# Attention values for four query blocks at once, in a fixed scheme over score steps

## The chip, the cores and the metric

The kernel runs on one core of a Trainium2 chip. The metric is device time in microseconds (us) of one execution. Engines are named as the profile names them: PE is TensorE's matmuls, PEld its weight loads, DVE VectorE, ACT ScalarE, POOL GpSimd and SP SyncE. POOL and SP issue DMAs here; POOL computes almost nothing.

## The reference

A small decoder trunk over 1,024 tokens of width 1,024, in float32: one short-convolution layer with a feed-forward part, then one layer of latent attention (8 heads) with a feed-forward part, then a norm. The change touches only the attention:

```
kv = (c_lat @ w_ukv)            # per head: 128 key columns, 128 value columns
q  = (cq @ w_uq)                # per head: 128 plain columns, 64 rotary columns
sc = q_nope . k_nope + q_pe . k_pe          # per block of 128 queries
p  = softmax(where(causal mask, sc * scale, -big))
attn = p @ v                                # per head
h  = h + attn @ w_o
```

With causal masking, query block qb (0 to 7, of 128 rows each) sees key blocks 0 to qb.

## The kernel before

Every float32 operand is split into two float32r parts, hi and lo (`split`, L93: a cast on ACT, L95, and a subtraction on DVE, L96). A product is three matmuls: hi by hi, hi by lo, lo by hi. Feature-major layout is used throughout: tokens lie along the free dimension, up to 512 columns for one matmul.

For each head h, four things are made ahead by projections: `make_k` (keys, 12 matmuls of 512 columns), `make_q` (plain queries, 18 of 512), and for two heads at a time `make_qr` (rotary queries, 18 of 512, then four rotary operations queued one by one and `done`, which moves the parts into place with DMAs on POOL) and `make_v` (values, 48 of 256). `wsplit` (L861) loads a projection's weights with a DMA on SP and splits them.

`scores` (L939) makes one query block: five terms in up to two pieces of 512 columns, a mask matmul (L948), a maximum on DVE (L950, L951), the exponential on ACT (L953, with its sum), and the scaling of the row on DVE (L954, L955). A score tile takes one PSUM bank (`ps1`, four buffers) up to 512 columns and two banks (`ps2`, two buffers) above. Projections use `ps2` too.

`pv` (L958) takes two query blocks (2i and 2i+1). It transposes their rows by key block on PE (L973, L974), two key blocks into one `ps1` bank, splits the bank into a `pt` tile (L95, L96), and then multiplies for each of its 2i+2 key blocks the value block's two parts with the 256 columns (128 at the last key block): L985, L986, L987. The output, 256 columns in its own `ps1` bank, is split, and stored to the DRAM tile `od` by POOL (`move`, L88), or kept in SBUF for the last two heads (`Od`).

The loop at L1036 runs over heads and over i = 0 to 3. Each round emits the scores of two blocks, then `pv` of the pair made two rounds earlier (`DEPTH` = 2), then a projection as the table `PLACES` (L40) says. In head 6 the outputs of heads 0 and 1 are loaded back (O0), in head 7 those of heads 2 to 5 (O1, eight loads of 512 KB on POOL, L1049). In these two heads `project_o` also makes the early part of the output projection, from heads 0 and 1, for all eight output blocks n, adding each into the residual block `h_of(n)`, which is itself loaded by a DMA on POOL. The remaining part follows after the loop (L1073).

SBUF tiles of 4 KB per partition come from one pool of 41 (`slot`). A planner orders the emitted instructions on each engine: the order of emission is their priority, and it takes those first that its own timing model holds to be ready. It also places all waits. On the chip each engine then runs its list in that order.

Of the kernel before, what the change touches and what calls it, by code (L numbers as in the profile page):

```python
# [10 lines left out]
F32 = mybir.dt.float32  # L11
F32R = mybir.dt.float32r
# [12 lines left out]
H = 8  # L25
# [2 lines left out]
QL = 384  # L28
EPS = 1e-6
SCALE = float((128 + ROPE) ** -0.5)  # L30
DEPTH = 2
NSLOT = 41
NHALF = 6
NRAW = 10
# [2 lines left out]
EARLY = 2  # L37
GROUPS = ((0, 1), (2, 3, 4), (5, 6, 7), (8, 9, 10))
KEPT = 4
PLACES = {0: ((0,), (1,), (), ()), 6: ((0,), (1,), (2, 3), (4,)), 7: ((0,), (1, 2), (3,), (4,))}  # L40
PLACES.update({h: ((0,), (1,), (2,), (3,)) if h % 2 else ((), (0,), (1,), ()) for h in range(1, 6)})
PREFETCH = 4
TC = {"schedule_with_timeline_sim": True}

# [13 lines left out]
def trunk(ctx, tc, aps, out):  # L58
# [22 lines left out]
    def ps2(name):  # L81
        return psum.tile([P, S], F32, name=name, tag="ps2", bufs=2)
# [786 lines left out]

    def make_k(h):  # L870
        w = wsplit("wk", w_ukv[:, :, h, 0:P], [P, 2, P])
        ps = ps2("ps_k")
        gemm(ps, w, lambda k: ch[k], lambda k: cl[k], range(2))
        kh, kl = slot("kh", F32R), slot("kl", F32R)
        split(kh, kl, ps)
        Kt[h] = (kh, kl)

    def make_v(h):

        raw = wraw("wv")  # L880
        dst = raw.rearrange("p (k h m) -> p k h m", k=2, h=2)
        for k in range(2):
            nc.sync.dma_start(dst[:, k], w_ukv[:, k, h:h + 2, P:2 * P])
        hi, lo = part(wop("wv"))
        split(hi, lo, raw)
        wh, wl = [t.rearrange("p (k m) -> p k m", k=2) for t in (hi, lo)]
        Vt[h], Vt[h + 1] = [(slot("vh", F32R), slot("vl", F32R)) for _ in range(2)]
        for t4 in range(2):
            ps = ps2("ps_v")
            for tb in range(4):  # L890
                tok = slice((t4 * 4 + tb) * P, (t4 * 4 + tb + 1) * P)
                o = ps[:, tb * 256:(tb + 1) * 256]
                for k in range(2):
                    nc.tensor.matmul(o, lhsT=ch[k][:, tok], rhs=wh[:, k, :], start=k == 0, stop=False)
                    nc.tensor.matmul(o, lhsT=ch[k][:, tok], rhs=wl[:, k, :], start=False, stop=False)
                    nc.tensor.matmul(o, lhsT=cl[k][:, tok], rhs=wh[:, k, :], start=False, stop=k == 1)
            pv_ = ps.rearrange("p (t h d) -> p t h d", h=2, d=P)
            for h2 in range(2):
                ov = lambda t: t[:, t4 * 512:(t4 + 1) * 512].rearrange("p (t d) -> p t d", d=P)
                split(ov(Vt[h + h2][0]), ov(Vt[h + h2][1]), pv_[:, :, h2, :])  # L900

    def make_q(h):
        w = wsplit("wqn", w_uq[:, :, h, 0:P], [P, 3, P])
        ps = ps2("ps_q")
        gemm(ps, w, lambda k: qh[k], lambda k: ql[k], range(3))
        a, b = slot("qnh", F32R), slot("qnl", F32R)
        split(a, b, ps)
        Qt.setdefault(h, {}).update(h=a, l=b)

    def make_qr(h):  # L910
# [6 lines left out]
        for k in range(3):  # L917
            rp = lambda t: t[:, k * P:(k + 1) * P].rearrange("p (q h f) -> p h q f", q=2, h=2, f=32)
            split(rp(hi), rp(lo), raw[:, k * P:(k + 1) * P].rearrange("p (h q f) -> p h q f", h=2, q=2, f=32))
        ps = ps2("ps_q")  # L920
        gemm(ps, lambda k: (hi[:, k * P:(k + 1) * P], lo[:, k * P:(k + 1) * P]),
             lambda k: qh[k], lambda k: ql[k], range(3))
# [16 lines left out]
    def scores(K, Q, qb, p):  # L939
        kw = (qb + 1) * P  # L940
        ps = ps2("ps_s") if kw > 512 else ps1("ps_s1")
        qs = slice(qb * P, kw)
        terms = ((Q["h"], K[0]), (Q["h"], K[1]), (Q["l"], K[0]), (Q["r"], KH), (Q["r"], KL))
        for i, (q, k) in enumerate(terms):
            for a in range(0, kw, 512):
                b = min(kw, a + 512)
                nc.tensor.matmul(ps[:, a:b], lhsT=q[:, qs], rhs=k[:, a:b], start=i == 0, stop=i == 4 and b < kw)  # L947
        nc.tensor.matmul(ps[:, qb * P:kw], lhsT=identr, rhs=cmask, start=False, stop=True)  # L948
        mx = small.tile([P, 1], F32, name="mx", bufs=4)
        nc.vector.reduce_max(mx, ps[:, :kw], axis=AX.X)  # L950
        nc.vector.tensor_scalar(mx, mx, nqscale[:, qb:qb + 1], None, ALU.mult)  # L951
        rsum = small.tile([P, 1], F32, name="rsum", bufs=4)
        nc.scalar.activation(p, ps[:, :kw], AF.Exp, bias=mx, scale=qscale[:, qb:qb + 1], accum_out=rsum)  # L953
        nc.vector.reciprocal(rsum, rsum)  # L954
        nc.vector.tensor_scalar(p, p, rsum, None, ALU.mult)  # L955
        return p

    def pv(V, i, pa, pb, h):  # L958
        nb = 2 * i + 2
        o = ps1("ps_pv")  # L960
        PT = []
        for _ in range(0, nb, 2):
            t = slot("pt", F32R)
            PT.append([t[:, a].rearrange("p (k q) -> p k q", q=256) for a in (T1, T2)])
        for kb in range(0, nb, 2):
            t = ps1("ps_t")
            tv = t.rearrange("p (k q) -> p k q", q=256)
            h_, l_ = PT[kb // 2]
            last = kb == nb - 2
            for j in range(2):  # L970
                ks = slice((kb + j) * P, (kb + j + 1) * P)
                if not (last and j == 1):
                    nc.tensor.transpose(tv[:, j, 0:P], pa[:, ks], ident)  # L973
                nc.tensor.transpose(tv[:, j, P:256], pb[:, ks], ident)  # L974
            if last:
                split(h_[:, 0, :], l_[:, 0, :], tv[:, 0, :])
                split(h_[:, 1, P:], l_[:, 1, P:], tv[:, 1, P:])
            else:
                split(h_, l_, tv)
        for kb in range(nb):  # L980
            h_, l_ = PT[kb // 2]
            vs = slice(kb * P, (kb + 1) * P)
            cs = slice(P, 256) if kb == nb - 1 else slice(0, 256)
            f, e = kb == 0, kb == nb - 1
            nc.tensor.matmul(o[:, cs], lhsT=V[0][:, vs], rhs=h_[:, kb % 2, cs], start=f, stop=False)  # L985
            nc.tensor.matmul(o[:, cs], lhsT=V[0][:, vs], rhs=l_[:, kb % 2, cs], start=False, stop=False)  # L986
            nc.tensor.matmul(o[:, cs], lhsT=V[1][:, vs], rhs=h_[:, kb % 2, cs], start=False, stop=e)  # L987
        if h in Od:
            split(Od[h][0][:, i * 256:(i + 1) * 256], Od[h][1][:, i * 256:(i + 1) * 256], o[:, :256])
            return  # L990
        ot = half("oh", F32R)
        oh, ol = ot[:, :256], ot[:, 256:]
        split(oh, ol, o[:, :256])
        move(od[h, 0, :, i * 256:(i + 1) * 256], oh)
        move(od[h, 1, :, i * 256:(i + 1) * 256], ol)

    make_k(0)
    make_qr(0)
    drip()
    make_q(0)  # L1000
    make_v(0)
    rq = rstd(q_acc, QL, pre=get_rs())
    qscale, nqscale = [const.tile([P, NT], F32, name=n) for n in ("qscale", "nqscale")]
    nc.vector.tensor_scalar(qscale, rq, SCALE, None, ALU.mult)
# [9 lines left out]

    st, h_of = stream(move)

    def project_o(O, k0, n):

        ps = ps2("ps_wo")
# [4 lines left out]
        hn = h_of(n)  # L1024
        nc.vector.tensor_tensor(hn, ps, hn, ALU.add)

    def p_tiles(i):
        a, b = (2 * i + 1) * P, (2 * i + 2) * P
        if a + b <= S:
            t = slot("p")  # L1030
            return t[:, :a], t[:, a:a + b]
        return slot("p")[:, :a], slot("p")[:, :b]

    Od = {}
    pend = []
    for h in range(H):  # L1036
        if h >= 6:
            Od[h] = (slot("oth", F32R), slot("otl", F32R))
        jobs = []
        if h + 1 < H:  # L1040
            jobs = [lambda h=h: make_k(h + 1), lambda h=h: make_q(h + 1)]
            if h % 2:
                jobs = [lambda: make_qr(h + 1), lambda: make_v(h + 1)] + jobs
        if h == H - 2:
            O0 = [load_o(k) for k in range(EARLY)]
        if h == H - 1:
            for n in range(3, 5):
                h_of(n)
            O1 = [load_o(k) for k in range(EARLY, 6)] + [Od[6], Od[7]]  # L1049
        if h >= H - 2:  # L1050
            early = range(KD)[:3] if h == H - 2 else range(KD)[3:]
            for n in early[:2]:
                h_of(n)
            jobs += [lambda n=n: project_o(O0, 0, n) for n in early]
        per = PLACES[h]
        for i in range(4):
            pa, pb = p_tiles(i)
            if i == 0:
                drip()
            for qb, p in ((2 * i, pa), (2 * i + 1, pb)):  # L1060
                scores(Kt[h], Qt[h], qb, p)
                drip(1)
            if len(pend) == DEPTH:
                pv(*pend.pop(0))
            pend.append((Vt[h], i, pa, pb, h))
            for j in per[i]:
                jobs[j]()
    for u in pend:
        pv(*u)


    X, final = next_operands(st, "mla_ffn_norm_g")
    for n in range(KD):  # L1073
# [104 lines left out]
```

## Time and profile before

| | us |
|---|---|
| median of three runs | 2125.18 (2120.62 to 2125.85) |
| the profiled execution, whole | 2121.5 |
| its span, first to last instruction | 2119.7 |
| PE busy | 2077.5 |
| DVE busy | 1627.7 |
| ACT busy | 935.5 |
| attention stage (1082.7 to 1403.1 of the span) | 320.4 |

In the profile a line gives an engine, a line of the kernel, an operation with output<-inputs (buffer numbers left out), and a count. Busy times of PE come from modelled ends of pipelined matmuls, so the spacing of starts says more than the durations. A wait is put down to the instruction that released it.

### The profile page before, as it was taken

What the parts mean: (1) busy time and instruction counts of PE and PEld (TensorE: products, weight loads), DVE (VectorE), ACT (ScalarE), POOL (GpSimd) and SP (SyncE); (2) the same over time, 40 slices, a digit from 0 to 9 for tenths busy, and PEclk for the clock granted to TensorE, in tenths of its full rate; (3) what the DMA queues carried; (4) which work ended last, traced back from release to release, by engine and by line L of the source; (5) the groups of instructions that cost most, each with busy time, mean ns of one, the idle gap of its engine ahead of it and who ended that gap; (6) DMA issues with size and microseconds to landing.
All of it is one profiled execution on the core that took longest, in us unless ns stands there. A gap on an engine that the chain in (4) does not pass through costs nothing.

```text
span 2119.7 us, 27634 instructions
## 1 busy us (share of the span) xinstructions
PE 2077.5 (98%) x9798; PEld 1730.1 (82%) x9798; DVE 1627.7 (77%) x2694; ACT 935.5 (44%) x1729; POOL 245.2 (12%) x464
## 2 busy tenths in 40 slices
PE   8999999999999999999999999999999999999998
PEld 6878887888888878888888888887888888878886
DVE  5697757789988887689467767767888888887785
ACT  6633344444444453224345545445444444443235
POOL 1000100000101121110002022100001010121100
PEclk9999999999999999999999999999999999999998
DMA  6133462343545587865222124522445445685851
GB/s 246 35 96 119 145 208 92 122 147 127 179 139 168 178 305 236 272 220 156 62 52 68 38 63 124 170 82 85 128 134 175 141 159 154 199 285 195 292 186 80
DMA packets 266858, 321.28 MB, mean 152 GB/s; under 512 B 19343, under 2 KB 214096, under 8 KB 266720
## 3 DMA queue, kind: packets, MB, share of 16 engines
q0 software_dynamic: 61248, 201.46, 28.1%
q1 hardware_dynamic: 205472, 118.07, 19.0%
q8 instruction: 77, 1.26, 0.2%
q14 instruction: 61, 0.50, 0.1%
HBM read 206.22 MB, written 108.00 MB: 148 GB/s over the span
## 4 chain that ended last, share of the span: by engine, by line
PE 88%; DVE 6%; DMA 2%; ACT 2%; issue 2%; SPq 0%; POOL 0%; POOLq 0%; ACTq 0%; DVEq 0%
PE ps_z L183 35%; PE ps_y L183 26%; PE ps_c L228 7%; PE ps_s L947 4%; PE ps_wo L108 1%; PE ps_wo L110 1%; PE ps_wo L112 1%; PE ps_l L112 1%; PE ps_l L108 1%; PE ps_l L110 1%; PE ps_pv L985 1%; PE ps_pv L986 1%; DMA w<-in_conv_ffn_w_dram 1%; PE ps_pv L987 1%; PE ps_q L108 1%
## 5 line engine op out<-in xcount | busy, mean ns | idle before, releaser
L183 PE MATMUL ps_z<-x,wo 128*128 128x512 f32 x2532 | 608.7, 389 | 3.6 <-ACT z L197 2.8
L183 PEld LDWEIGHTS ps_z<-x,wo 128*128 128x128 f32 x2532 | 474.6, 188 | 104.4 <-ACT z L197 4.1
L183 PE MATMUL ps_y<-x,wo 128*128 128x512 f32 x1764 | 432.3, 389 | 1.2 <-DVE x L96 0.9
L183 PEld LDWEIGHTS ps_y<-x,wo 128*128 128x128 f32 x1764 | 330.5, 188 | 70.9 <-DVE x L96 1.8
L95 ACT CAST wo<-w 128x512 fp32r<-128x512 f32 (+2 forms) x423 | 238.7, 570 | 278.0 <-PE ps_z L183 109.0
L96 DVE TENSOR_TENSOR wo<-w,wo 128x512 fp32r<-128x512 f32 (+2 forms) x423 | 260.4, 622 | 61.9 <-ACT wo L95 61.0
L183 PE MATMUL ps_z<-xm,wo 128*128 128x512 f32 x960 | 239.0, 392 | 4.2 <-ACT wo L95 1.6
L183 PEld LDWEIGHTS ps_z<-xm,wo 128*128 128x128 f32 x960 | 178.6, 188 | 46.3 <-DVE h L503 3.4
L95 ACT CAST wo<-sums 128x512 fp32r<-128x512 f32 (+2 forms) x172 | 98.3, 572 | 256.7 <-PE ps_y L183 101.5
L183 PE MATMUL ps_y<-xm,wo 128*128 128x512 f32 x720 | 181.6, 390 | 2.0 <-DVE h L503 2.0
L88 POOL DMA_DIRECT2D md<-x x140 | 74.9, 536 | 737.8 <-DVE x L96 704.8
L183 PEld LDWEIGHTS ps_y<-xm,wo 128*128 128x128 f32 x720 | 134.7, 188 | 31.0 <-DVE h L503 2.9
L197 ACT COPY z<-ps_z 128x512 f32<-128x512 f32 x106 | 62.0, 585 | 136.6 <-PE ps_z L183 136.5
L96 DVE TENSOR_TENSOR wo<-sums,wo 128x512 fp32r<-128x512 f32 (+2 forms) x172 | 107.2, 623 | 14.3 <-ACT wo L95 12.7
L88 POOL DMA_DIRECT2D xm<-md x140 | 74.1, 535 | 251.3 <-PE ps_z L183 126.3
L503 DVE TENSOR_TENSOR h<-ps_z,h 128x512 f32<-128x512 f32 x104 | 71.4, 687 | 36.5 <-PE ps_z L183 35.7
L96 DVE TENSOR_TENSOR x<-t,x 128x512 fp32r<-128x512 f32 x136 | 92.0, 684 | 5.1 <-ACT x L95 5.1
L237 DVE TENSOR_TENSOR a<-ps_y,z 128x512 f32<-128x512 f32 x88 | 60.6, 688 | 42.4 <-PE ps_y L183 42.1
L95 ACT CAST x<-t 128x512 fp32r<-128x512 f32 x136 | 82.4, 621 | 20.9 <-DVE t L252 20.3
L953 ACT ACTIVATE p<-ps_s,mx,qscale 128x128 f32<-128x128 f32 (+3 forms) x64 | 53.4, 835 | 82.4 <-DVE mx L951 80.0
L158 DVE TENSOR_TENSOR sums<-w,w 128x512 f32<-128x512 f32 (+2 forms) x85 | 53.2, 626 | 29.4 <-DMA w<-in_mla_ffn_w_dram 13.4
L503 DVE TENSOR_TENSOR h<-ps_y,h 128x512 f32<-128x512 f32 x88 | 60.2, 685 | 19.9 <-PE ps_y L183 19.8
(297 smaller groups left out, 3344.8 us busy)
## 6 DMA issues: line engine op xcount, KB each, us to landing
md<-x POOLq DMA_DIRECT2D x140, 512.0 KB, 3.6
xm<-md POOLq DMA_DIRECT2D x140, 512.0 KB, 8.1
w<-in_conv_ffn_w_dram SPq DMA_DIRECT2D x88, 256.0 KB, 2.8
w<-in_mla_ffn_w_dram SPq DMA_DIRECT2D x88, 256.0 KB, 3.0
w<-in_conv_w_in_dram SPq DMA_DIRECT2D x48, 256.0 KB, 3.0
hd<-h POOLq DMA_DIRECT2D x24, 512.0 KB, 3.6
w<-in_conv_ffn_w_dram SPq DMA_DIRECT2D x48, 192.0 KB, 4.9
w<-in_mla_ffn_w_dram SPq DMA_DIRECT2D x48, 192.0 KB, 4.5
```

The costliest lines, as they stand in the source:

```text
L88: nc.gpsimd.dma_start(dst, src)
L95: nc.scalar.copy(out=hi, in_=src)
L96: (eng or nc.vector).tensor_tensor(lo, src, hi.bitcast(F32), ALU.subtract)
L108: nc.tensor.matmul(ps[:, hs], lhsT=wh, rhs=xh(k)[:, hs], start=st, stop=False)
L158: tt(sums, R["12"], R["22"], ALU.add)
L183: mm = lambda w_, x_, f: nc.tensor.matmul(b, lhsT=w_[:, m], rhs=x_, start=f, stop=True, skip_group_check=True)
L197: nc.scalar.copy(out=kept[name], in_=b)
L228: nc.tensor.matmul(ps[:, ts], lhsT=w_[:, m], rhs=X[i][f"b{kh}{th}"][:, q, :], start=st and j == 0, stop=en and j == 2)
L237: nc.vector.tensor_tensor(dst, ps, add, ALU.add)
L503: nc.vector.tensor_tensor(dst[name], b, dst[name], ALU.add)
L947: nc.tensor.matmul(ps[:, a:b], lhsT=q[:, qs], rhs=k[:, a:b], start=i == 0, stop=i == 4 and b < kw)
L953: nc.scalar.activation(p, ps[:, :kw], AF.Exp, bias=mx, scale=qscale[:, qb:qb + 1], accum_out=rsum)
```

## The change

`pv` is split into three functions that the loop calls piecemeal. A group g is four query blocks: group 0 is blocks 0 to 3 with four key blocks, group 1 blocks 4 to 7 with eight. `turn(kb)` transposes key block kb of all query blocks that see it into one bank and returns the function that splits it. `add(kb)` does the three matmuls for one key block, with 512 columns (384, 256, 128 on the diagonal). `out_` splits 512 output columns. The loop runs over steps t = 8h + qb; two key blocks are turned in each step from the second after a group's last scores, and added two steps later. `scores` now returns the exponential part and the scaling, which the loop emits a step later. Projections are generators: the part up to the first `yield` (weight load and split, and for an early output part the load of its residual block) is emitted a step ahead of the rest. They stand at set steps: in even heads keys at block 0 and queries at block 2; in odd heads rotary queries at 0, values at 1 and 2, keys at 3, queries at 6. The early output parts stand at three steps of head 6, three of head 7, and two after it.

```diff
-DEPTH = 2
-PLACES = {0: ((0,), (1,), (), ()), 6: ((0,), (1,), (2, 3), (4,)), 7: ((0,), (1, 2), (3,), (4,))}
-PLACES.update({h: ((0,), (1,), (2,), (3,)) if h % 2 else ((), (0,), (1,), ()) for h in range(1, 6)})
...
     def make_k(h):
         w = wsplit("wk", w_ukv[:, :, h, 0:P], [P, 2, P])
+        yield
         ps = ps2("ps_k")
...
         for t4 in range(2):
+            yield
             ps = ps2("ps_v")
...
-        mx = small.tile([P, 1], F32, name="mx", bufs=4)
-        nc.vector.reduce_max(mx, ps[:, :kw], axis=AX.X)
-        nc.vector.tensor_scalar(mx, mx, nqscale[:, qb:qb + 1], None, ALU.mult)
-        rsum = small.tile([P, 1], F32, name="rsum", bufs=4)
-        nc.scalar.activation(p, ps[:, :kw], AF.Exp, bias=mx, scale=qscale[:, qb:qb + 1], accum_out=rsum)
-        nc.vector.reciprocal(rsum, rsum)
-        nc.vector.tensor_scalar(p, p, rsum, None, ALU.mult)
-        return p
-
-    def pv(V, i, pa, pb, h):
...
+        mx, rsum = [small.tile([P, 1], F32, name=n, bufs=4) for n in ("mx", "rsum")]
+
+        def exp():
+            nc.vector.reduce_max(mx, ps[:, :kw], axis=AX.X)
+            nc.vector.tensor_scalar(mx, mx, nqscale[:, qb:qb + 1], None, ALU.mult)
+            nc.scalar.activation(p, ps[:, :kw], AF.Exp, bias=mx, scale=qscale[:, qb:qb + 1], accum_out=rsum)
+
+        def scaled():
+            nc.vector.reciprocal(rsum, rsum)
+            nc.vector.tensor_scalar(p, p, rsum, None, ALU.mult)
+
+        return exp, scaled
+
+    def pv(V, g, p, h):
+
+        nb, q0 = 4 * g + 4, 4 * g
+        PT, O = {}, []
+
+        def turn(kb):
+            t, o_ = ps1("ps_t"), slot("pt", F32R, [P, 2, HS])
+            j0 = max(0, kb - q0)
+            for j in range(j0, 4):
+                nc.tensor.transpose(t[:, j * P:(j + 1) * P], p[j][:, kb * P:(kb + 1) * P], ident)
+            cs = slice(j0 * P, HS)
+            PT[kb] = o_, cs
+            return lambda: split(o_[:, 0, cs], o_[:, 1, cs], t[:, cs])
+
+        def add(kb):
+            if kb == 0:
+                O.append(ps1("ps_pv"))
+            o, (o_, cs) = O[0], PT.pop(kb)
+            vs = slice(kb * P, (kb + 1) * P)
+            for i, (v, q) in enumerate(((0, 0), (0, 1), (1, 0))):
+                nc.tensor.matmul(o[:, cs], lhsT=V[v][:, vs], rhs=o_[:, q, cs], start=kb == 0 and i == 0, stop=kb == nb - 1 and i == 2)
+
+        def out_():
+            ts = (T1, T2)[g]
+            if h in Od:
+                split(Od[h][0][:, ts], Od[h][1][:, ts], O[0])
             else:
...
+                oh, ol = half("oh", F32R), half("ol", F32R)
+                split(oh, ol, O[0])
+                move(od[h, 0, :, ts], oh)
+                move(od[h, 1, :, ts], ol)
+
+        return turn, add, out_
...
+    def project_early(n):
+        hn = h_of(n)
+        w = wsplit("wo", w_o[:, 0:EARLY, n * P:(n + 1) * P], [P, EARLY, P])
+        yield
+        ps = ps2("ps_wo")
+        gemm(ps, w, lambda k: O0[k][0], lambda k: O0[k][1], range(EARLY))
+        nc.vector.tensor_tensor(hn, ps, hn, ALU.add)
...
+    def place(h, qb, job):
+
+        t = h * NT + qb
+        jobs.setdefault(t - 1, []).append(job)
+        for i in range(2 if job.gi_code.co_name == "make_v" else 1):
+            jobs.setdefault(t + i, []).append(job)
+
+    for h in range(H - 1):
+        if h % 2:
+            for qb, job in enumerate((make_qr(h + 1), make_v(h + 1))):
+                place(h, qb, job)
+        place(h, 3 if h % 2 else 0, make_k(h + 1))
+        place(h, 6 if h % 2 else 2, make_q(h + 1))
+    for n, (h, qb) in enumerate(((6, 3), (6, 5), (6, 7), (7, 0), (7, 1), (7, 2), (8, 0), (8, 1))):
+        place(h, qb, project_early(n))
...
+    for t in range(H * NT + 7):
+        h, qb = t // NT, t % NT
+        if h < H:
...
+            exp, scaled = scores(Kt[h], Qt[h], qb, p[qb % 4])
+        for f in splits:
+            f()
+        splits = []
+        if h < H:
+            exp()
+        now = units.pop(t, ())
+        for f in now:
+            if f[0] == "turn":
+                splits.append(f[1]())
+        for f in now:
+            if f[0] == "add":
+                f[1]()
+        if last_scaled:
+            last_scaled()
+        last_scaled = scaled if h < H else None
+        for f in now:
+            if f[0] == "out":
+                f[1]()
+        drip(1)
+        run_jobs(t)
+        if qb % 4 == 3 and h < H:
+            turn, add, out_ = pv(Vt[h], qb // 4, p, h)
+            nb = 4 * (qb // 4) + 4
+            for kb in range(nb):
+                units.setdefault(t + 2 + kb // 2, []).append(("turn", lambda kb=kb, f=turn: f(kb)))
+            for kb in range(nb):
+                units.setdefault(t + 4 + kb // 2, []).append(("add", lambda kb=kb, f=add: f(kb)))
+            units[t + 3 + nb // 2].append(("out", out_))
```

## Rows read from the trace of the kernel before

**Rows 1.** The page, parts 1 and 4: busy time, chain that ended last.

```profile
PE 2077.5 (98%) x9798; PEld 1730.1 (82%) x9798; DVE 1627.7 (77%) x2694; ACT 935.5 (44%) x1729; POOL 245.2 (12%) x464
...
PE 88%; DVE 6%; DMA 2%; ACT 2%; issue 2%; SPq 0%; POOL 0%; POOLq 0%; ACTq 0%; DVEq 0%
```

**Rows 2.** Busy time by stretch: from:to, length, each engine busy (instructions), clock, DMA.

```profile
1082.70:1131.06 48.36, 47.64 (x317) 43.21 (x315) 37.22 (x95) 26.93 (x62) 6.79 (x14) 1.00 0.24 62
1131.06:1205.01 73.95, 71.44 (x456) 63.59 (x456) 54.35 (x122) 37.75 (x87) 13.06 (x24) 1.00 0.22 55
...
1352.50:1403.10 50.60, 48.34 (x288) 41.86 (x286) 27.33 (x55) 18.19 (x43) 1.05 (x2) 1.00 0.16 52
```

**Rows 3.** PE in order of time: start us, duration us, line, operation, count.

```profile
1151.75 0.62 PE L112 MATMUL ps_k<-lat_hi,wk 128*128 128x512 f32 x2
1152.21 0.28 PE L985 MATMUL ps_pv<-pt,vh 128*128 128x256 f32 x1
1152.32 0.28 PE L986 MATMUL ps_pv<-pt,vh 128*128 128x256 f32 x1
1152.44 0.28 PE L987 MATMUL ps_pv<-pt,vl 128*128 128x256 f32 x1
...
1155.42 0.27 PE L974 MATMUL ps_t<-ident,p 128*128 128x128 f32 x1
1155.53 0.27 PE L973 MATMUL ps_t<-ident,p 128*128 128x128 f32 x1
...
1159.84 0.34 PE L947 MATMUL ps_s<-kl,qnh 128*128 128x384 f32 x1
...
1160.19 0.33 PE L947 MATMUL ps_s<-KH,qrs 128*128 128x384 f32 x1
```

**Rows 4.** Weight loads' waits, 1082 to 1404: us in total, times, longest.

```profile
PEld ps_s L947 <- ACT p L953: 4.7, 5, 1.7
PEld ps_pv L985 <- ACT p L953: 3.0, 5, 0.7
PEld ps_k L108 <- ACT p L953: 2.4, 4, 0.8
PEld ps_t L973 <- DVE oh L96: 1.9, 3, 0.8
...
PEld ps_t L973 <- DVE pt L96: 0.6, 2, 0.3
...
PEld ps_t L973 <- ACT p L953: 0.4, 2, 0.2
```

**Rows 5.** Groups by form on PE, 1083 to 1401: busy us, mean ns.

```profile
L985 PE MATMUL ps_pv<-pt,vh 128*128 128x256 f32 x128 | 38.4, 300 | 2.0 <-ACT p L953 1.8 <-DVE pt L96 0.2
...
L985 PE MATMUL ps_pv<-pt,vh 128*128 128x128 f32 x32 | 7.3, 228 | 0.0
```

**Rows 6.** Groups by form on DVE and ACT, 1131.06 to 1205.01.

```profile
L96 DVE TENSOR_TENSOR pt<-ps_t,pt 128x512 fp32r<-128x512 f32 x12 | 8.1, 686 | 0.6 <-ACT pt L95 0.6
...
L950 DVE TENSOR_REDUCE mx<-ps_s 128x1 f32<-128x1024 f32 x2 | 2.4, 1220 | 1.6 <-PE ps_s L948 1.6
...
L96 DVE TENSOR_TENSOR pt<-ps_t,pt 128x128 fp32r<-128x128 f32 x8 | 2.2, 281 | 0.0
...
L955 DVE TENSOR_SCALAR p<-p,rsum 128x1024 f32<-128x1024 f32 x2 | 1.5, 754 | 0.1
...
L95 ACT CAST pt<-ps_t 128x512 fp32r<-128x512 f32 x12 | 6.8, 582 | 1.1 <-PE ps_t L974 0.8
...
L953 ACT ACTIVATE p<-ps_s,mx,qscale 128x1024 f32<-128x1024 f32 x2 | 2.4, 1210 | 4.2 <-DVE mx L951 4.2
```

**Rows 7.** POOL in order of time: issues of residual blocks, then O1's eight.

```profile
1328.41 1.60 POOL L88 DMA_DIRECT2D h<-hd  x3
...
1337.05 0.53 POOL L88 DMA_DIRECT2D otl<-od  x1 [0.52 <-DMA h<-hd]
```

**Rows 8.** Tile oth: time from issue to landing of its loads.

```profile
DMA to landing us min/median/max: 5.1/8.4/11.7
```

More of the change, by code (lines that the diff above doesn't have):

```diff
@@ L919, in make_qr @@
             split(rp(hi), rp(lo), raw[:, k * P:(k + 1) * P].rearrange("p (h q f) -> p h q f", h=2, q=2, f=32))
+        yield
         ps = ps2("ps_q")
@@ L956, in scores @@
-        return p
-    def pv(V, i, pa, pb, h):
[L959 to L977, printed above, removed]
-            else:
[L979 to L995, printed above, removed]
@@ L997, in trunk @@
-    make_k(0)
-    make_qr(0)
+        mx, rsum = [small.tile([P, 1], F32, name=n, bufs=4) for n in ("mx", "rsum")]
[6 more added lines that the diff above has]
+            nc.vector.tensor_scalar(p, p, rsum, None, ALU.mult)
@@ L999, in trunk, with whole @@
+    def whole(job):
+        for _ in job:
+            pass
+    whole(make_k(0))
+    whole(make_qr(0))
     drip()
-    make_q(0)
-    make_v(0)
+    whole(make_q(0))
+    whole(make_v(0))
     rq = rstd(q_acc, QL, pre=get_rs())
@@ L1015, in trunk @@
     st, h_of = stream(move)
+    def project_early(n):
+        hn = h_of(n)
+        w = wsplit("wo", w_o[:, 0:EARLY, n * P:(n + 1) * P], [P, EARLY, P])
+        yield
+        ps = ps2("ps_wo")
+        gemm(ps, w, lambda k: O0[k][0], lambda k: O0[k][1], range(EARLY))
+        nc.vector.tensor_tensor(hn, ps, hn, ALU.add)
     def project_o(O, k0, n):
@@ L1025, in project_o @@
         nc.vector.tensor_tensor(hn, ps, hn, ALU.add)
[L1027 to L1032, printed above, removed]
-    Od = {}
[L1035 to L1058, printed above, removed]
-                drip()
[L1060 to L1067, printed above, removed]
@@ L1068, in trunk, with p_tiles @@
-    for u in pend:
-        pv(*u)
+    def p_tiles(g):
+        if g:
+            return [slot("p")[:, :(qb + 1) * P] for qb in range(4, 8)]
+        t = slot("p")
+        return [t[:, :P], t[:, P:3 * P], t[:, 3 * P:6 * P], slot("p")[:, :4 * P]]
+    Od = {}
+    jobs = {}
+    def place(h, qb, job):
[3 more added lines that the diff above has]
+            jobs.setdefault(t + i, []).append(job)
@@ new lines, in trunk, with run_jobs @@
+    for h in range(H - 1):
[6 more added lines that the diff above has]
+        place(h, qb, project_early(n))
+    def run_jobs(t):
+        for job in jobs.pop(t, ()):
+            next(job, None)
+    run_jobs(-1)
@@ new lines, in trunk @@
+    units, splits, last_scaled = {}, [], None
+    for t in range(H * NT + 7):
+        h, qb = t // NT, t % NT
+        if h < H:
+            if qb == 0:
+                drip()
+                if h >= 6:
+                    Od[h] = (slot("oth", F32R), slot("otl", F32R))
+                if h == H - 2:
+                    O0 = [load_o(k) for k in range(EARLY)]
+                if h == H - 1:
+                    O1 = [load_o(k) for k in range(EARLY, 6)] + [Od[6], Od[7]]
+            if qb % 4 == 0:
+                p = p_tiles(qb // 4)
+            exp, scaled = scores(Kt[h], Qt[h], qb, p[qb % 4])
[27 more added lines that the diff above has]
+            units[t + 3 + nb // 2].append(("out", out_))
```

## Prediction

> **What bounds the kernel now.** Read the page first: TensorE (PE) is busy in 98% of the span and holds 88% of the chain that ended last [rows 1]. The change touches one stage only, the attention between the latent products and the output projection, so the next view is the busy time by stretches of it [rows 2]: about 320 us from 1082.7 to 1403.1, in which eight heads run. Heads repeat in pairs, because the rotary queries and the values are made for two heads at a time. One pair lasts 73.95 us, with 456 matmuls. PE is shown busy for 71.4 us of it, VectorE (DVE) for 54.4, ScalarE (ACT) for 37.8. A busy PE is not yet a PE at its rate, so the third view is PE's own order of time [rows 3], read from start to start: a matmul of 512 columns takes 0.23 us (two in 0.46), 384 columns 0.175 (two in 0.35), 256 columns 0.12 (0.11 and 0.12 in the rows; 0.12 over the six that follow each other), 128 columns 0.11 (the transposes). Each matmul loads its own weights, and below 256 columns it no longer gets cheaper.
>
> With these prices the pair can be added up from the code. 512 columns: 60 in scores, 24 for keys, 36 for queries, 18 for rotary queries, 138 x 0.23 = 31.7. 384: 20 x 0.175 = 3.5. 256: 20 in scores, 96 in attention values, 48 for V, 164 x 0.12 = 19.7. 128: 36 in scores and masks, 72 transposes, 24 in attention values, 132 x 0.112 = 14.8. The sum is 69.7 us for 454 matmuls, so a pair of 73.95 us holds some 4.2 us in which PE waits. The waits by who waited for whom [rows 4] give the same from the other side: the weight loads of the stage waited 18.9 us in 14 rows (the first five of interest and the last are shown), most of it for an exponential (ACT p) that still holds a PSUM buffer. A weight load waits ahead of its matmul, partly beside the one before, so the true loss is less; from the pairs (three times 4.2, and a little at each end) I take 14 us for the stage. PE's work is then about 306 us and its stalls 14. That is all that a better order can give; the rest must come from cheaper matmuls.
>
> **Part 1: the values for four query blocks.** In the kernel before, a head does 20 key-block steps of three matmuls, 48 with 256 columns and 12 with 128 (the stage's rows of one of the three lines: 128 and 32 [rows 5]). After, per head, group 0 has four key blocks and group 1 eight, with 512 columns wherever all four query blocks see the key block: 18 matmuls of 512, 6 of 384, 6 of 256, 6 of 128. The columns are the same 13,824; the count falls from 60 to 36, 480 to 288 in all. Price per head: before 48 x 0.12 + 12 x 0.112 = 7.10; after 18 x 0.23 + 6 x 0.175 + 6 x 0.12 + 6 x 0.112 = 6.58. Saved 0.52, in eight heads **4.2 us**, all on PE and so on the path. The price of a matmul with 512 columns that this rests on is from projections, which do the same thing. The Trainium skill, TensorE: Matmul & The Clock Gate, section Back-to-back issue gap, puts a warm matmul at N/2.4 + 2.5 ns, so 109 ns for 256 columns and 216 for 512; the rows stand 10 and 14 ns above that. By that and the same page's section LDWEIGHTS (128 columns in 107 ns, the floor for the small ones), the saving would be an estimated 2.8 us in place of 4.2, and the time 2116.
>
> The 36 transposes per head are the same, just grouped by key block. The copies out of PSUM (hi cast on ACT, remainder on DVE) go from 14 per head (six of 512 columns, four of 256, four of 128) to 12 (six, two of 384, two of 256, two of 128), and the outputs from four of 256 to two of 512. On DVE, at 0.69 and 0.28 us for 512 and 128 columns [rows 6] and 0.55 and 0.42 on the line between, that is 6.9 + 1.7 before and 6.6 + 1.4 after, 0.6 us less per head; ACT gains about as much. Neither engine is full [rows 2], so nothing is booked. Stores of outputs fall from 48 to 24 at twice the size, on POOL, which nobody waits for: nothing.
>
> **Part 2: the order.** A step is one query block's scores. In it the planner now gets, in falling priority: scores, copies of the last step's transposes, maximum and exponential, two key blocks' transposes, the matmuls of two key blocks turned two steps ago, then the scaling of the step before, then a projection. The planner still sorts by its own clock, so these are priorities. What it does to the waits of [rows 4], row by row. Keys waiting for an exponential (2.4): in odd heads they were made behind query block 5, where scores hold both of the two-bank buffers; now behind block 3, whose scores use one bank. Gone. Transposes waiting for an output copy (1.9): half as many outputs, half gone. Values waiting for an exponential's bank (3.0): 16 output banks are opened in place of 32, half gone. Scores waiting for an exponential (4.7): the same double buffer stays, half gone at best. Scores that wait for a new query or value copy (some 2 in the rows not shown): queries are made one or more blocks earlier, half gone. That is 2.4 + 1 + 1.5 + 2.3 + 1 = 8.2 us of weight-load waits; at 14 us true for 18.9 shown, **6 us**. The bounds are 0 (each wait comes back elsewhere) and 14.
>
> **Part 3: what could wait anew.** (a) A group's first transposes need the scaled row of its last query block. Maximum 1.22, exponential 1.21, scaling 0.75 [rows 6] and the small ones come to about 3.7 us; two steps lie between, with at least 1.2 + 0.7 + 0.7 + 2.8 + 0.7 = 6 us of PE work. Covered; if not, at most 1 us per head. (b) One-bank buffers are four: a score tile, the value accumulator and two transposes. From the third to the sixth step of a head the new transposes need the banks of the last step's, which must be copied first: 0.58 + 2 x 0.69 = 2 us [rows 6], against at least 1.38 of value matmuls and 1.0 to 1.9 of scores between. Covered by half a microsecond; before, this wait is 0.6 us in the whole stage [rows 4]. Uncovered, it is up to 0.69 in each of 32 steps, 22 us. I take 0, the row nearest to it. (c) Weight loads of a projection are issued and split one step ahead: SP carries only such loads in this stage, so nothing is passed, and the splits are the same ones. Nothing. (d) On POOL, residual block 4 for the early output parts was loaded ahead of the eight loads of O1 (blocks 2 to 4 at 1328.4, the last of the eight at 1337.1 [rows 7]) and block 5 behind; now both stand behind. Those eight landed after up to 11.7 us [rows 8]. Block 4's addition on DVE comes about 8 us after the first of them, and its data perhaps 12 to 15 after. Behind it on DVE are maxima and copies, for which PE waits. Between 0 (the planner places the addition later) and 7 us; I take 0. (e) The slot pool of 41 fills up to about 41 in head 7 by the code; before, POOL waited there too without harm to PE. Nothing. (f) The work after the last scores grows to seven steps, but the last two early parts (5.5 us) and the first projections with all inputs but the last head's (13.8) fill it. Nothing.
>
> **Sum.** The profiled execution took 2121.5 us for a span of 2119.7, which is 3.7 us under the median of the three runs shown. 2121.5 - 4.2 - 6 = 2111.3; against the median, 2125.2 - 10.2 = **2115**. A difference of 0.3%, 6.4 us, is about what a measurement of this kernel can tell from no change.
>
> **Rivals.** *All stalls go*: 2125.2 - 4.2 - 14 = 2107. For it: DVE has 26% of a pair free, every distance in the new scheme is two steps. Against: two two-bank buffers still serve scores and projections. *The stalls move*: only the 4.2 us stay, 2121, within 0.3%. For it: the planner re-sorts whatever order it is given by a clock that is not the chip's, so that the fixed steps aren't kept to; then the change doesn't do what it says. *The residual loads hold DVE* (d): 2115 + 4 to 7, 2120, within 0.3%. It decides if block 4 lands later than the planner believed. The Trainium skill, TensorE: Matmul & The Clock Gate, section on the architectural detail of the array, says that ScalarE and VectorE take their queues strictly in order; by that, a late addition stops every maximum behind it. No row here shows DVE waiting for such a load. *The one-bank buffers bind* (b), the slower side: if DVE runs half a microsecond late in the steps where transposes follow transposes, PE waits up to 0.69 in each of 32, 22 us; with two thirds of that and the old stalls still there, 2125.2 - 4.2 + 14 = 2135. For it: in the third step of an odd head DVE has two transposes' copies and two V copies (4 x 0.69), a rotary product (1,024 columns, about 1.2 like the maximum of as many) and some 1.1 of maximum and scaling, 5.1 us by [rows 6], against 1.0 of scores, 0.9 of transposes and 2.9 of V on PE, 4.8. Against: value matmuls whose copies are ready can be taken first.
>
> **How the numbers follow.** Forecast 0.42 (its own range 2109 to 2121, about 0.36 of it beyond 0.3%), all stalls gone 0.15, stalls moved 0.22, residual loads 0.08, one-bank buffers 0.13. Faster: 0.36 + 0.15 = 0.51; within 0.3%: 0.06 + 0.22 + 0.08 = 0.36; slower 0.13. The range runs from 2105 to 2128: it leaves out a little of the second case and nearly all of the last.
>
> **What would show it.** In the changed kernel's forms, 48 rows' count of 512 columns on each value line at 0.23 us from start to start; 9606 matmuls on PE; a pair of heads at 70 to 71.5 us; weight loads' waits in the stage at 10 to 12 us, those of keys for an exponential gone. It is wrong if 512-column value matmuls are spaced wider than 0.23, if transposes wait for copies for more than 3 us in total (case b), or if a DVE addition in heads 6 and 7 waits for a load (case d).

## The result and the profile after

The changed kernel takes 2104.9 us (median of four runs, 2104.2 to 2110.0), against 2123.8 for the kernel before: 18.9 us less by the medians; the ratio of the runs is 0.9917, 95% interval 0.9898 to 0.9936. The direction was forecast; the size was forecast at 10, and the time lies just under the range that began at 2105. It is the first rival, the one in which all stalls go, that came closest (2107); how much of that closeness is luck is said below.

The page of the changed kernel, parts 1 and 4, for [rows 1]:

```profile
PE 2071.3 (98%) x9606; PEld 1721.6 (82%) x9606; DVE 1624.9 (77%) x2662; ACT 932.0 (44%) x1697; POOL 230.5 (11%) x440
...
PE 92%; DVE 3%; DMA 2%; ACT 1%; issue 1%; SPq 0%; POOL 0%; POOLq 0%; DVEq 0%; ACTq 0%
```

PE has 192 matmuls fewer, as forecast, and the chain that ended last runs through PE for 92% of the span where it was 88%; DVE's part in it has halved. The page says no more, since a busy PE is not a PE at its rate.

The stage, from its first score to its last value matmul, in one line: the length, then each engine busy (instructions). The kernel before in its second profile, then the changed one:

```profile
1084.36:1401.15 316.79, 307.69 (x1904) 271.73 (x1903) 224.65 (x499) 151.73 (x344) 53.50 (x99) 1.00 0.30 85
```

```profile
1085.44:1380.77 295.33, 294.57 (x1702) 257.48 (x1702) 220.74 (x467) 147.81 (x312) 38.82 (x75) 1.00 0.30 91
```

The stage fell from 316.8 to 295.3 us. PE showed 9.1 us of it idle before, and 0.8 after. Some matmuls of the output projection fall within the stage, 158 before and 148 after, the early parts' 96 among them; with 148 in each, the stage went from 314.5 to 295.3, 19.2 us less.

PE in order of time in the changed kernel, value matmuls of group 1 of heads 0, 2 and 4, each of which runs during the head after, for [rows 3]:

```profile
1131.42 0.68 PE L983 MATMUL ps_pv<-pt,vh 128*128 128x512 f32 x2
...
1198.99 0.40 PE L983 MATMUL ps_pv<-pt,vl 128*128 128x512 f32 x1
1199.23 0.62 PE L983 MATMUL ps_pv<-pt,vh 128*128 128x512 f32 x2
1199.69 0.39 PE L983 MATMUL ps_pv<-pt,vl 128*128 128x512 f32 x1
1199.92 0.39 PE L983 MATMUL ps_pv<-pt,vh 128*128 128x512 f32 x1
...
1268.52 0.68 PE L983 MATMUL ps_pv<-pt,vh 128*128 128x512 f32 x2
```

From start to start a value matmul of 512 columns takes 0.23 us (1198.99 to 1199.23 rounds to 0.24, two in 0.46, one in 0.23), the price that the sum had taken from projections. The first and the last line are the same place two pairs of heads apart: 137.1 us, 68.55 a pair, where the prediction looked for 70 to 71.5. The sum by prices for a pair was 69.7 before, and is 1.05 less now, 68.65. So a pair of heads runs at its price, with nothing left over; before it took 73.95 [rows 2].

The weight loads' waits in the stage, all that the changed kernel has, for [rows 4]:

```profile
PEld ps_s L948 <- DVE kl L93: 1.3, 2, 0.6
PEld ps_wo L105 <- DVE h L1037: 1.1, 1, 1.1
PEld ps_v L893 <- DVE qnl L93: 0.6, 1, 0.6
PEld ps_s L948 <- DVE h L1027: 0.2, 1, 0.2
PEld ps_pv L983 <- DVE pt L93: 0.2, 1, 0.2
PEld ps_s L948 <- DVE qnl L93: 0.2, 1, 0.2
```

Six rows and 3.6 us where fourteen with 18.9 stood and 10 to 12 were forecast. Not one wait for an exponential (ACT p) is left, neither of scores nor of values nor of keys, and none of a transpose for a copy.

**A measure for the experiments.** PE's work in the stage is added up from the counts of its matmuls and the prices of the prediction (0.23, 0.175, 0.12, 0.112 us); what the stage lasts beyond that is called its rest. Counted are the matmuls that start between the first score and the last value matmul; the counts in the lines above take in two neighbours more. For the kernel before: 662 matmuls of 512 columns (158 of them the output projection's), 80 of 384, 632 of 256, 528 of 128 make 301.2 us, so the rest is 15.5 of 316.7. Changed: 796, 128, 296 and 480 make 294.8, a rest of 0.6. (The rest falls to -1.4 in one run, so its zero is good to about 1.5 us.) "Behind" is the span from the last value matmul on; stage and "behind" are both brought to 148 projection matmuls in the stage, at 0.23 us each.

| kernel | median us | ratio to before, interval | stage | rest | behind |
|---|---|---|---|---|---|
| before, two profiles | 2123.8 | 1 | 314.4, 314.5 | 15.5, 15.6 | 722.3, 723.3 |
| changed, two profiles | 2104.9 | 0.9917 (0.9898 to 0.9936) | 295.3, 295.3 | 0.6, 0.6 | 727.2, 726.7 |
| e1 halves | 2108.9 | 0.9931 (0.9919 to 0.9944) | 299.9 | 1.1 | 724.1 |
| e2 old places | 2124.0 | 0.9996 (0.9987 to 1.0006) | 312.4 | 17.6 | 730.2 |
| e3 same step | 2116.8 | 0.9969 (0.9956 to 0.9981) | 306.2 | 11.4 | 726.1 |
| e4 places alone | 2118.9 | 0.9971 (0.9959 to 0.9982) | 309.6 | 10.6 | 721.9 |
| e7 keys, queries old | 2109.3 | 0.9943 (0.9928 to 0.9958) | 301.7 | 7.0 | 722.9 |
| e8 rotary, values old | 2117.8 | 0.9975 (0.9963 to 0.9986) | 305.8 | 11.0 | 730.3 |
| e9 copies now | 2101.9 | 0.9905 (0.9883 to 0.9926) | 293.4 | -1.4 | 727.2 |
| e10 scale now | 2104.2 | 0.9899 (0.9883 to 0.9916) | 295.3 | 0.5 | 726.6 |
| e11 copies, even pieces | 2103.6 | 0.9900 (0.9886 to 0.9915) | 291.9 | -0.8 | 726.3 |

In e11 a matmul of 320 columns counts 0.145 us, from its rows below. A profiled execution can lie 4 to 5 us off its kernel's median (e2 and e8 above, e4 below), but the stage repeats within 0.1 us: three profiles of the same instructions, the changed kernel's two and e10's, show 295.3.

So the 19.2 us of the stage are 4.2 of PE's work (301.2 less 294.8, less the ten projection matmuls) and 15 of stalls. The first is what was forecast, the second is two and a half times it. The experiments ask what took the stalls away.

### The profile page after: what moved, and what is told of

The parts are those of the page before. It is cut to its first block, busy times and chain, and to the rows that moved or that the text cites. A ratio compares the mean times of both kernels' runs of the same rounds, so it can differ in the third digit from the quotient of the medians.

```text
span 2108.0 us, 27158 instructions
## 1 busy us (share of the span) xinstructions
PE 2071.3 (98%) x9606; PEld 1721.6 (82%) x9606; DVE 1624.9 (77%) x2662; ACT 932.0 (44%) x1697; POOL 230.5 (11%) x440
## 4 chain that ended last, share of the span: by engine, by line
PE 92%; DVE 3%; DMA 2%; ACT 1%; issue 1%; SPq 0%; POOL 0%; POOLq 0%; DVEq 0%; ACTq 0%
PE ps_z L180 37%; PE ps_y L180 27%; PE ps_c L225 7%; PE ps_s L948 4%; PE ps_pv L983 2%; PE ps_t L972 1%; PE ps_wo L105 1%; PE ps_wo L107 1%; PE ps_wo L109 1%; PE ps_l L109 1%; PE ps_l L105 1%; PE ps_l L107 1%; DMA w<-in_mla_ffn_w_dram 1%; PE ps_q L105 1%; PE ps_q L107 1%
## 5 line engine op out<-in xcount | busy, mean ns | idle before, releaser
L500 DVE TENSOR_TENSOR h<-ps_z,h 128x512 f32<-128x512 f32 x104 | 71.5, 688 | 40.5 <-PE ps_z L180 39.6
```

The lines of the kernel that those rows point to most:

```text
L500: nc.vector.tensor_tensor(dst[name], b, dst[name], ALU.add)
```

## The experiments

Two theories: "distance" (transposes, copies and value matmuls stand in steps of their own, two apart) and "places" (the projections stand where they hold nobody up). A third thing, the wide matmul itself, is to be kept out.

### e1: only the width undone

```diff
-            for i, (v, q) in enumerate(((0, 0), (0, 1), (1, 0))):
-                nc.tensor.matmul(o[:, cs], ...)
+            for i, (v, q) in enumerate(((0, 0), (0, 1), (1, 0))):
+                for a, z in ((0, HS),) if kb == 0 and i == 0 else ((0, 256), (256, HS)):
+                    c = slice(max(a, cs.start), z)
+                    if c.start < z:
+                        nc.tensor.matmul(o[:, c], ...)
```

> The changed kernel with each value matmul cut into two of at most 256 columns (the first of each group stays whole); steps and projections as changed. 176 more matmuls. By the prices read from start to start (0.23, 0.175, 0.12, 0.11 us for 512, 384, 256, 128 columns) PE's work grows by 0.50 us per head, 4 us. Theory 'distance' (the two steps between transposes, copies and value matmuls took the stalls away) and theory 'places' (the new places of the projections did) both expect just that: 2109 us, and a stage with PE stalls of 1 to 3 us as in the changed kernel. If the wide matmuls themselves took the stalls away, some of the 15 us come back too: 2115 to 2124.

Measured 2108.9, the stage 4.6 us longer than in the changed kernel, and its rest 0.5 us more. The width is worth about what the prices say, 4.0 us, and no stall of size depends on it. With the formula for a matmul by itself, the Trainium skill (TensorE: Matmul & The Clock Gate, sections Back-to-back issue gap and LDWEIGHTS) gives an estimated 2.8 us for the same cut; the trace stands nearer to its own rows. The prediction used that formula for a stream in which each matmul loads its own weights.

### e2 and e4: one of the two parts alone

e2 keeps the new values and steps, and puts the projections back to the blocks where they were:

```diff
-            for qb, job in enumerate((make_qr(h + 1), make_v(h + 1))):
+            for qb, job in ((1, make_qr(h + 1)), (3, make_v(h + 1))):
                 place(h, qb, job)
-        place(h, 3 if h % 2 else 0, make_k(h + 1))
-        place(h, 6 if h % 2 else 2, make_q(h + 1))
-    for n, (h, qb) in enumerate(((6, 3), (6, 5), (6, 7), (7, 0), (7, 1), (7, 2), (8, 0), (8, 1))):
+        place(h, 5 if h % 2 else 3 if 0 < h < 6 else 1, make_k(h + 1))
+        place(h, 7 if h % 2 else 5 if 0 < h < 6 else 3, make_q(h + 1))
+    for n, (h, qb) in enumerate(((6, 5), (6, 5), (6, 7), (7, 1), (7, 3), (7, 3), (7, 5), (7, 7))):
```

> The changed kernel with its projections and early output parts emitted behind the query blocks where the kernel before has them (in odd heads rotary queries at block 1, values at 3, keys at 5, queries at 7; in even heads keys at 3, queries at 5); values for four blocks and their steps stay. Theory 'places': the waits of keys, queries and scores for a two-bank buffer come back, 8 to 12 us, so 2113 to 2117. Theory 'distance': these waits stay away, 2105 to 2108.

Measured 2124.0: no gain is left at all, worse than either theory had it. In the profiles 17.1 us of the loss are in the stage and some 3 behind it. The stage and PE's longest waits in it:

```profile
1083.57:1395.97 312.40, 300.10 (x1702) 257.93 (x1702) 218.70 (x467) 145.44 (x312) 40.06 (x75) 1.00 0.28 86
```

```profile
PE ps_pv L983 <- ACT pt L92: 5.6, 6, 1.3
PE ps_q L105 <- ACT p L955: 1.6, 2, 0.8
PE ps_s L948 <- ACT p L955: 1.3, 3, 0.5
```

With the same matmuls as the changed kernel, 12.3 us of PE idle stand in the first line. Value matmuls now wait for the copies of their transposes, a wait that neither the kernel before nor the changed one has in this size, although they are still emitted two steps later. So the distance alone does not hold: six of the 96 groups of value matmuls start within 0.5 us of the end of ACT's copy, and none in the changed kernel.

e4 is the kernel before with only the new places (and the weights a step ahead): values for two blocks, emitted in one piece two rounds late.

```diff
-            turn, add, out_ = pv(Vt[h], qb // 4, p, h)
...
+        if qb % 2:
+            if len(pend) == 2:
+                pv(*pend.pop(0))
+            pend.append((Vt[h], qb // 2, pa, pb, h))
+        run_jobs(t)
```

> The kernel before with only the projections' new places and their weights a step ahead: values for two query blocks at once, all emitted behind the scores, two rounds late, as before. PE's work is that of before. Theory 'places': 8 to 12 us of the 15 us of stalls go, 2112 to 2116. Theory 'distance': 2120 to 2124.

Measured 2118.9, between the two. The rest falls from 15.5 to 10.6. What is left is for the most part transposes and projections that wait for an exponential:

```profile
PE ps_t L978 <- ACT p L955: 3.5, 3, 1.6
PE ps_wo L105 <- ACT p L955: 1.9, 2, 1.6
PE ps_s L948 <- DVE mx L954: 1.7, 2, 0.9
```

Set in a square, the rest is 15.5 with both old, 10.6 with the new places alone, 17.6 with the new values alone, 0.6 with both. One part gives 4.9 us, the other -2.1; together they give 15. Neither theory is right by itself. (The square is not quite clean: e2 and e4 both have the weights a step ahead, which the kernel before has not, and no run tells that apart.)

### e7 and e8: which places

The edits of e2, taken apart; first e7:

```diff
-        place(h, 3 if h % 2 else 0, make_k(h + 1))
-        place(h, 6 if h % 2 else 2, make_q(h + 1))
+        place(h, 5 if h % 2 else 3 if 0 < h < 6 else 1, make_k(h + 1))
+        place(h, 7 if h % 2 else 5 if 0 < h < 6 else 3, make_q(h + 1))
```

> The changed kernel with only the keys and plain queries emitted at the old blocks (odd heads 5 and 7, even heads 3 and 5, head 0 at 1 and 3); rotary queries, values and early output parts at the new ones. Theory 'two-bank buffers': keys and queries then share the two double banks with the scores of blocks 4 to 7, and PE waits for exponentials that hold them: most of the 17 us that the old places cost together come back, 2115 to 2124. Theory 'DVE load': what costs is the V copies and the rotary products falling into the steps full of transposes' copies: 2105 to 2110 here.

and e8:

```diff
-            for qb, job in enumerate((make_qr(h + 1), make_v(h + 1))):
+            for qb, job in ((1, make_qr(h + 1)), (3, make_v(h + 1))):
```

> The changed kernel with only the rotary queries and the values emitted at the old blocks of the odd heads (1, and 3 with 4); keys, queries and early output parts at the new ones. Theory 'two-bank buffers': 2105 to 2110. Theory 'DVE load': 2113 to 2122, with value matmuls waiting for pt in the trace.

Measured: 2109.3 with keys and queries back (rest 7.0), 2117.8 with rotary queries and values back (rest 11.0). Over the changed kernel's 0.6 that is 6.4 and 10.4, together 16.8 of e2's 17.0, so the two add up, and the early output parts' places carry next to nothing. The longest waits of weight loads, of e7 and then of e8:

```profile
PEld ps_s L948 <- DVE kl L93: 4.0, 5, 1.0
PEld ps_q L105 <- ACT p L955: 1.8, 2, 0.9
PEld ps_pv L983 <- ACT pt L92: 1.4, 2, 0.7
```

```profile
PEld ps_s L948 <- ACT p L955: 3.7, 3, 1.3
PEld ps_s L948 <- DVE vl L93: 3.3, 3, 1.3
PEld ps_s L948 <- PE ps_pv L983: 1.9, 3, 0.6
```

The larger loss comes with rotary queries and values, as "DVE load" had it. That it does so because the values' four copies of 512 columns per half fall into the steps that already copy transposes is argued, not shown: e7 and e8 don't part the values from the rotary queries. In e7, too, the longest wait is for a copy on DVE (kl, the key's remainder), more than for an exponential in a two-bank buffer. That buffers count as well is seen in the second line of e7 and the first of e8. The value matmuls' wait for pt, which "DVE load" expected of e8, is not among its longest; the lateness shows at the scores.

### e3 and e9: the distance

```diff
-                splits.append(f[1]())
+                f[1]()()
...
-                units.setdefault(t + 4 + kb // 2, []).append(("add", lambda kb=kb, f=add: f(kb)))
-            units[t + 3 + nb // 2].append(("out", out_))
+                units.setdefault(t + 2 + kb // 2, []).append(("add", lambda kb=kb, f=add: f(kb)))
+            units[t + 1 + nb // 2].append(("out", out_))
```

> The changed kernel with no distance: two key blocks' transposes, their copies and their value matmuls are emitted in one and the same step. Matmuls and places of projections stay. Theory 'distance': a value matmul now waits for the copy made just before (0.58 on ACT, then 0.69 twice on DVE), unless the planner finds other work; 6 to 15 us more, 2111 to 2120, with value matmuls waiting for pt in the trace. Theory 'places': 2105 to 2107, since the planner fills the gap with projections and the next scores.

Measured 2116.8, a rest of 11.4, in the range of "distance". But the waits are not those expected:

```profile
PE ps_s L948 <- DVE kl L93: 3.3, 3, 1.3
PE ps_wo L105 <- ACT p L955: 1.9, 1, 1.9
...
PE ps_pv L983 <- DVE pt L93: 0.3, 1, 0.3
```

The planner saw that the value matmuls would not be ready and took other work; what is late is the next thing on DVE, the key copies, and an exponential at the end. PE's waits that the view names in this stage come to 8.4 us; the other 3 of the rest have no name.

e9 has the first line of that edit only: copies at once, value matmuls still two steps behind.

```diff
-                splits.append(f[1]())
+                f[1]()()
```

> The changed kernel with each pair of transposes copied in its own step instead of the next one (ahead of nothing but behind the maximum and exponential of that step); the value matmuls stay two steps behind. Theory 'distance of the value matmuls': no change beyond 2 us, 2104 to 2107. Rival 'the copies' place on DVE and ACT': with the copies not first in the next step, the order on DVE changes as it did where everything was in one step, and key and query copies come late: 2110 to 2117.

Measured 2101.9, and the stage 1.9 us shorter than in the changed kernel, with these the longest waits of weight loads left:

```profile
PEld ps_wo L105 <- DVE h L1037: 1.1, 1, 1.1
PEld ps_v L893 <- DVE qnl L93: 0.6, 1, 0.6
```

So of the two things that e3 undoes, it is the value matmuls' distance that counts. That the copies wait for the next step gains nothing.

### e10: the scaling at its old place

> The changed kernel with each row scaled on DVE right behind its exponential instead of a step later. Theory 'distance of the value matmuls': transposes come two steps after the last score either way, so no change beyond 2 us, 2103 to 2107. Rival: DVE takes its list in order, the scaling waits there for the exponential (up to 1.4 us for one of 1,024 columns with its sum), and the copies and maxima behind it come late: 2108 to 2120, with DVE waiting for ACT p in the trace.

```diff
             exp()
+            scaled()
...
-        if last_scaled:
-            last_scaled()
-        last_scaled = scaled if h < H else None
```

Measured 2104.2, a rest of 0.5. DVE's longest wait in the stage is the one behind the exponential that the rival feared, and it is the same line, word for word, in the changed kernel:

```profile
DVE rsum L958 <- ACT p L955: 19.9, 26, 1.4
```

The two traces show the same instructions in the same order on every engine. So the planner places the scaling where its clock says, whichever step it is emitted in; that part of the scheme does nothing, and the rival was not put to the test.

### e11: what is left to gain

The first edit of e3, and in `scores` for 640 keys

```diff
+        if kw == 640:
+            ps = ps[:, 192:192 + kw]
+        cut = 320 if kw == 640 else 512
```

with pieces of `cut` columns.

> A version meant to beat both: the changed kernel with copies of transposes in their own step (as in e9_copies_now), and the scores over 640 keys cut into two pieces of 320 columns in place of 512 and 128. With no stalls left in the stage only PE's work can give more: five terms in eight heads, 0.23 + 0.11 us by two of about 0.15 (between 256 columns at 0.12 and 384 at 0.175), 0.04 us each, 1.6 us. So 2100 to 2101 against 2101.9 of e9_copies_now; the stage 1.6 us shorter. If the small piece's weight load was hidden anyway: the same as e9_copies_now.

The five terms of such a score, in order of time:

```profile
1197.66 0.45 PE L951 MATMUL ps_s<-kh,qnh 128*128 128x320 f32 x2
1197.95 0.46 PE L951 MATMUL ps_s<-kl,qnh 128*128 128x320 f32 x2
1198.24 0.46 PE L951 MATMUL ps_s<-kh,qnl 128*128 128x320 f32 x2
```

Two pieces take 0.29 us against the 0.34 of 512 and 128. The stage is 1.5 us shorter than in e9, where 1.6 was worked out, but the time, 2103.6, is no different from e9's or from the changed kernel's within the intervals. No version here beats the changed kernel by more than can be measured.

### e5 and e12: both kernels once more

> The changed kernel once more, unaltered, for a second profile: the first profiled execution took 2110.0 us, 5 more than its other runs, with single waits of up to 3 us for DVE in the feed-forward parts that the change does not touch. Expected if those 5 us are the execution's own: 2104 to 2106, the attention stage 295 us as before. If they belong to the kernel: 2109 to 2110 again.

> The kernel before, unaltered, for a second profile. In its first profile the work behind the attention stage took 722 us (with 150 of the output projection's matmuls counted to the stage); in five profiles of the changed kernel and its near variants it took 727 to 728, with waits of 3 us for DVE behind a weight load and a granted clock of 0.97 around them. If those 5 us belong to the changed schedule, 722 again here and no stretch of 50 us under 0.99; if they are the executions' own, up to 727. The attention stage: 316 to 317 us, PE's waits in it 16 us.

The changed kernel took 2109.8 again under the profile, but e10, with the same instructions in the same order, took 2104.7. In these three profiles the stage begins at 1085.4, 1085.7 and 1081.0; from there on they agree within 0.6 us. So the 5 us lie ahead of the stage and belong to the execution. In all thirteen profiles the stage begins between 1080.9 and 1085.7, and differences of that size cannot be put down to the change.

What lies behind the stage differs more steadily: 722.3 and 723.3 us for the kernel before, 727.2, 726.7 and 726.6 for the changed one and e10, 727.2 and 726.3 for e9 and e11. PE's longest waits there, changed and before (second profile):

```profile
PE ps_z L180 <- DVE h L500: 3.0, 1, 3.0
PE ps_y L180 <- DVE h L500: 2.0, 1, 2.0
```

```profile
PE ps_y L183 <- DVE h L503: 1.8, 1, 1.8
PE sp L1104 <- DVE o L1120: 1.6, 1, 1.6
```

DVE in its turn waited longer there for weights of the second feed-forward part, up to 4.5 us at once against 2.4:

```profile
DVE sums L155 <- DMA w<-in_mla_ffn_w_dram: 14.8, 8, 4.5
```

```profile
DVE sums L158 <- DMA w<-in_mla_ffn_w_dram: 9.5, 8, 2.4
```

The last figure, the longest of these waits, is the one that counts. In all thirteen profiles PE's wait in `ps_z` for `h` is 1.5 or 1.6 us shorter than it, and what lies behind the stage follows: PE waits 0.8 and 0.9 us in the kernel before (722.3, 723.3 behind), 1.2 and 1.5 in e7 and e4 (722.9, 721.9), 1.8 to 2.2 in e1, e3 and e11 (724.1 to 726.3), 2.9 to 3.4 in the changed kernel, e10 and e9 (726.6 to 727.2), 3.9 and 5.2 in e2 and e8 (730.2, 730.3). So about 4 us of the 19 are given back, around one weight load that lands late, in a part that the change doesn't touch. Why that load lands later is not settled, and it does not go with the length of the stage: e2 and e4 have 312 and 310 us there, and 730 and 722 behind. No run held the second part fixed while the first was changed.

## Why the prediction was right or wrong

**Right.** The matmuls: 9606; 512 columns at 0.23 us; 4.2 us of work less (e1: 4.6 for undoing nearly all of it, where the same prices give 4.0). The covers: (a) and (b) of Part 3 hold, no transpose waits for a scaled row or for a copy's bank; (c), (e) and (f) cost nothing in the stage. The early additions (d) waited for no load and held a weight load up for 0.2 us in all. The slower rival, the one-bank buffers, did not come.

**Wrong: the size of the stalls' term.** The 14 us that Part 2 had to give were 15, well read. What failed is the step that went through [rows 4] row by row and let each wait go by half, or wholly, on a reason of its own, to 6 us. It treated the waits as separate. The square of e2 and e4 shows that they are not: a rest of 15.5 with both parts old, 10.6 and 17.6 with one, 0.6 with both.

What the traces show in place of Part 2's reasons is room on PE's side, and no faster help. An exponential ends on average 3.01 us after its score's last matmul in the changed kernel and 2.86 before (64 of each; the longest 6.2 and 5.5), so DVE and ACT answer no sooner than they did. But what needs an answer stands farther behind it: from the end of DVE's part of a `pt` copy to the first matmul that reads it the median is 3.8 us, where it was 1.9, and one of 96 has less than 0.5 us, where 12 of 160 had. PE finds other ready work in between. With the projections at their old places (e2) the exponentials end 3.45 us after their scores, and the copies come too late for the two steps. Which copies on DVE and ACT make them late there was not tested. "Two two-bank buffers still serve scores and projections", the argument against the first rival, was no obstacle: with the new places, no wait for an exponential is left.

**Wrong: nothing booked behind the stage.** The sum took all that lies behind as unchanged; it took about 4 us more. Had both been sized right, the sum would have been 2123.8 - 4.2 - 15 + 4 = 2108.6; the median is 3.7 lower, less than the part ahead of the stage differs between executions of the same instructions. So it is in part luck that the first rival's time came so near: it had the stage right, and what it left out on either side nearly cancelled.

**The second rival, that the planner undoes the fixed scheme,** is right in one point: the scaling stands where the planner's clock puts it (e10). That the copies wait a step makes another order, but gains nothing (e9). What the planner did not undo are the places of the projections and the distance of the value matmuls.

## What to carry to other kernels

Add up the bottleneck engine's work from counts and start-to-start prices first; what the stage lasts beyond it is the most that order can give. Don't share that amount out wait by wait: an order that leaves the bottleneck engine ready work wherever a helper engine's answer is still out can take all the waits, without the helper being any faster, and half of such an order may take none (17.6 against 15.5). And measure what lies behind the stage as well: here it gave back about 4 us of 19, for a reason that stayed open.

## What the runs showed of the hardware that was not expected

A wait of PE can cost more than its own length. In the changed kernel PE waited 2.0 us for DVE in the second feed-forward part, up to 1870.5. Stretches around it: length, engines busy, and in the third figure from the end the granted clock:

```profile
1864.00:1867.00 3.00, 3.00 (x14) 2.44 (x13) 3.00 (x7) 2.49 (x6) 1.06 (x2) 1.00 1.11 395
1867.00:1870.50 3.50, 1.52 (x7) 0.94 (x5) 2.10 (x5) 1.66 (x3) 1.48 (x3) 1.00 1.13 386
1870.50:1872.00 1.50, 1.46 (x4) 1.23 (x5) 1.50 (x4) 0.00 (x0) 0.46 (x2) 0.64 1.16 381
1872.00:1874.00 2.00, 2.00 (x6) 1.54 (x6) 2.00 (x5) 0.00 (x0) 0.17 (x1) 0.50 1.13 387
1874.00:1876.00 2.00, 2.00 (x10) 1.60 (x9) 1.57 (x4) 1.27 (x3) 0.00 (x0) 0.92 1.12 389
```

The clock fell to 0.64 and 0.50 (the lower of its two levels, 1.2 GHz) just as PE went on, and was back in the third stretch: 1.5 x 0.36 + 2 x 0.50 + 2 x 0.08 = 1.7 us lost beyond the wait. The length of a wait does not tell whether this follows. In the same profile the 3.0 us wait for `h` was followed by 2 us at 0.50; in e10, with the same instructions in the same order and the same wait of 3.0 us, the clock stayed at 1.00 around it. The stage itself kept a granted clock of 1.00 in every kernel here, with waits of PE of up to 1.9 us among them (e3).
